# A stick-breaking branch moved ahead of the first gate, with paced weight sums, in a hybrid decoder layer

## The chip, the cores and the metric

The kernel runs on one core of a Trainium2 chip. The metric is device time in microseconds of one execution; the median of several runs is compared. TensorE (PE) multiplies matrices, VectorE (DVE) and ScalarE (ACT) do elementwise work, GpSimd (POOL) and SyncE (SP) mostly start DMAs here.

## The reference

One layer for 512 tokens of width 1024 in float32. A combined projection of `x` feeds three causal token mixers and three gates; the gated sum goes through an output projection and a LayerNorm, and an MLP with a gated extra embedding and a second LayerNorm follows:

```python
o_da = diff_attention(...)            # 4 heads, two softmax maps each
o_sb = stick_breaking_attention(...)  # 8 heads
o_dl = dilated_attention(...)         # 3 groups of 4 heads
g = jax.nn.sigmoid(gates).reshape(B, S, N_BRANCHES, D)
merged = (g[:, :, 0] * (o_da @ w_branch_da) + g[:, :, 1] * (o_sb @ w_branch_sb)
          + g[:, :, 2] * (o_dl @ w_branch_dil))
x = layer_norm(DEEPNORM_ALPHA * x + merged @ w_out, ln1_g, ln1_b)
c = jnp.square(jax.nn.relu(x @ w_up)) @ w_down
ple = jax.nn.sigmoid(x @ w_ple_gate) * (p @ w_ple)
x = layer_norm(DEEPNORM_ALPHA * x + c + ple, ln2_g, ln2_b)
```

The part of differential attention that the change touches, for every head and block of 128 queries:

```python
prob = jax.nn.softmax(logits, axis=-1)
w = prob[:, :, 0] - lam * prob[:, :, 1]
o = einsum(w, v)
o = o * lax.rsqrt(jnp.mean(jnp.square(o), axis=-1, keepdims=True) + RMS_EPS) * norm_g * (1 - lam_init)
```

## The kernel before, in words

**Products in three parts.** A float32 product is made of three matmuls of a faster type: every operand is split into a high part (a cast) and a low part (the rest), and high x high, high x low and low x high are summed in PSUM. Each 128x1024 chunk of weights is therefore loaded on SP's queue into `raw` (7 buffers), cast by ScalarE into `wh` (line 212) and subtracted by VectorE into `wl` (line 214); `wh` and `wl` have 6 buffers each. `pump` keeps these stages ahead of the matmuls that read them.

**Products with fewer multiplications.** The dilated values, the three gates, the gate of the extra embedding and most of the MLP use a two-by-two scheme of seven products in place of eight (Winograd's). It needs sums of blocks of weights and of activations. The sums of weights (`vsum`, `msum`, `gsum`, `usum`, `dsum`) are made in device memory by DMAs of 512 KB on POOL's queue, some of which add into their target: `sum_steps` yields 200 of them, eight for each group, up to four groups taking turns. The sums of activations are "forms": `value_forms` makes them for the dilated values from loads called `xr` (line 347), `mixer_forms` for the gates from loads also called `xr` (line 331); each makes eight such loads.

**Items.** TensorE's work is a list of items, each 12 to 24 matmuls with an evacuation `ev`. Items 0 to 64 are projections and values (`t_item`, `v_items`, `value_pair`); `last_plain` is 65. Then come the first gate (`gate_alone`, 14 items, line 575 ff.), the stick-breaking branch (`branch_items(1)`, 8 items, line 634 ff.), the second gate and the dilated branch, the third gate and the differential branch, the output projection, the extra embedding and the MLP, 298 items in all. The gate of a branch is a sigmoid (`gate_sig`, line 499), called one item ahead of the branch item (`pre`); the branch item's `ev` multiplies it by the branch product from PSUM (line 651). The first branch starts the sum `merged`, the others add to it.

**What runs between items.** The attention heads are generators. `step` advances those that are active, once per item and once more in the middle of projections and values; a head may start when the PSUM banks that the active ones declare leave room. All eight stick-breaking heads come first, then dilated and differential ones. Before the last item of the first gate the loop calls `step` until no head is left:

```python
if n == branch_at[1] - 1:
    while active or waiting:
        step()
```

`mixer_forms` is started at `last_plain - 5`. `split_oT(i)` splits a branch's attention outputs two items before the branch. The weight sums are issued by a credit: every item adds its size times a rate (2.6 up to `last_plain`, then 1.4, none around the output projection, later 0.42), and each whole unit issues one sum. An order derived from this program by a planner, which models times and hands out buffers, is what the engines run; each engine then works in that order. Most 128x512 tiles come from one pool of 46 buffers (`slot`), PSUM has 2 banks `mm` and 6 banks `at`.

**A block of differential attention** (`da_block`): logits of two maps, bias and maximum (line 1583), two exponentials with row sums (1589), reciprocals of the sums, one times lambda (1592, 1593), the second map scaled (1594), the first scaled and added (1595). Three steps later the result is transposed (1600) and copied, two steps later multiplied by the values (1614) and the squares summed (1618). After the last block of a head: `pow` on POOL (1624), scaling (1627), transposes (1633), `oT`.

Of the kernel before, what the change touches and what calls it, by code (L numbers as in the profile page):

```python
# [55 lines left out]
def trunk(tc, a, out):  # L56
    nc = tc.nc
    es = ExitStack()
    with es:
# [335 lines left out]
        def value_pair(nv):  # L395
# [6 lines left out]
            for p in (2, 1, 7, 6, 4, 5, 3):  # L402
                for r in range(2):
# [20 lines left out]
                    def ev(ps, p=p, r=r):  # L424
# [14 lines left out]
                        else:  # L439
                            o = V["dl_v", 2, r + 2 * (p == 5)] = slot("dl_v") if p == 4 else s[7, r]  # L440
                            nc.vector.scalar_tensor_tensor(o, s[7, r], -1.0, ps, op0=OP.mult, op1=OP.subtract)
                    item(cs[p] if r else [], mm, ev, need=cs[p], bank=bank, size=0.5)

        def v_items(nv, name, g):
            cs = [chunk(a["wv"][nv, c].rearrange("p k n -> p (k n)"), 1024) for c in range(4)]
            for tt in range(4):
# [11 lines left out]
                def ev(ps, tt=tt):  # L458
# [8 lines left out]
                    else:  # L467
                        t = slot(name)
                        cp(t, ps)
                        V[name, g, tt] = t  # L470
                item(cs if tt == 3 else [], mm, ev, need=cs)

        nt, nv = 2, 0
# [63 lines left out]
        def seven(forms, operand, bank_of, done):  # L537

            cs = {}
            for p in (2, 1, 7, 6, 4, 5, 3):  # L540
                for r in range(2):
# [19 lines left out]
                    if p == 5:  # L561
                        bank_of.get("sums", set()).add(len(items))
                    item(cs[p] if r else [], mm, ev, need=cs[p], bank=bank, size=0.5)

        msum = [[[dram.tile([P, 1024], F32, name=f"msum{n}_{m}_{i}") for i in range(4)] for m in range(2)]
# [68 lines left out]
        def branch_items(i, behind=()):  # L634
            behind = list(behind)
            for half in range(2):
                cs = [chunk(a["wb"][i, half, c].rearrange("p k n -> p (k n)"), 1024) for c in range(2)]
                for tt in range(4):
                    def mm(ps, tt=tt, cs=cs):
                        q = slice(tt * P, tt * P + P)  # L640
                        for k in range(4):
                            c = cs[k // 2]
                            n = slice(k % 2 * 512, k % 2 * 512 + 512)
                            h, lo = oTs[4 * i + k]
                            nc.tensor.matmul(ps, h[:, q], c["h"][:, n], start=k == 0, stop=False)  # L645
                            nc.tensor.matmul(ps, h[:, q], c["l"][:, n], start=False, stop=False)  # L646
                            nc.tensor.matmul(ps, lo[:, q], c["h"][:, n], start=False, stop=k == 3)  # L647

                    def ev(ps, tt=tt, half=half):
                        g = sg.pop((i, tt, half))  # L650
                        nc.vector.tensor_mul(g, g, ps)
                        if i == 1:
                            merged[tt, half] = g
                        else:
                            nc.vector.tensor_add(merged[tt, half], merged[tt, half], g)

                    def pre(tt=tt, half=half):
                        sg[i, tt, half] = gate_sig(i, tt, half)
                    item(cs if tt == 3 else [], mm, ev, need=cs, bank=at_bank, size=0.5)
                    items[-1]["pre"] = pre  # L660
                    if half and behind:
                        behind.pop(0)()
# [15 lines left out]
        last_plain = len(items)  # L678
        gate_alone(0, 1)
        branch_at = {1: len(items)}  # L680
        branch_items(1)
        for n, i in ((1, 2), (2, 0)):
            gate_chain(n, i)
            branch_at[i] = len(items)
            branch_items(i, () if i else [lambda k=k: turn_item(k) for k in range(4)])
# [255 lines left out]
        def sum_steps():  # L941
# [36 lines left out]
            todo.extend(up_steps(gsum[m], a["wg"][m]) for m in range(2))  # L978
            for m in range(ND):
                todo.append(up_steps(usum[m], a["wu"][m]))  # L980
                if m < ND - 1:
                    todo.append(down_steps(m))
            run = []
            while todo or run:
                while todo and len(run) < 4:
                    run.append(todo.popleft())
# [581 lines left out]
        da_po = {}  # L1568
        da_ss = {}
        da_left = {}  # L1570

        def da_block(hd, qb):
# [15 lines left out]
            for m in range(2):  # L1588
                e = nc.scalar.activation(lg[m], lg[m], AF.Exp, bias=mx[:, m:m + 1], accum_out=ssum[:, m:m + 1])
                last_exp[0] = getattr(e, "ins", e)  # L1590
            r = small("rr", 2)
            nc.vector.reciprocal(r, ssum)
            nc.vector.tensor_mul(r[:, 1:2], r[:, 1:2], lam)
            nc.vector.tensor_scalar(lg[1], lg[1], r[:, 1:2], None, op0=OP.mult)
            nc.vector.scalar_tensor_tensor(lg[0], lg[0], r[:, 0:1], lg[1], op0=OP.mult, op1=OP.add)
            for _ in range(3):
# [20 lines left out]
            ss = da_ss[hd]  # L1617
            nc.scalar.activation(scr, po[:, qs], AF.Square, accum_out=ss[:, qb:qb + 1])
            da_left[hd] -= 1
            if da_left[hd] == 0:  # L1620
                yield

                nc.vector.tensor_scalar(ss, ss, 1.0 / P, EPS, op0=OP.mult, op1=OP.add)
                nc.gpsimd.tensor_tensor(ss, ss, mhalf.to_broadcast([P, 4]), OP.pow)
                yield
                on = slot("on")
# [188 lines left out]
        sum_steps_ = sum_steps()  # L1815
        RATES = 2.6, 1.4
        credit = 0.0
        plain_left[0] = last_plain
        forms_at = last_plain - 5
        freed = 8  # L1820
        prev = None
        for n, it in enumerate(items):
            if n == v_from[0]:
                pending.append(value_forms())
            if n == forms_at:
                pending.append(mixer_forms())
            if n == branch_at[1] - 1:
                while active or waiting:
                    step()
# [28 lines left out]

            if 12 <= n < wout_at - 6:
                credit += it["size"] * (RATES[0] if n < last_plain else RATES[1])  # L1860
            elif n > ple_at + 14:
                credit += 0.42
            while credit >= 1:
# [141 lines left out]
```

## Time and profile before

| | |
|---|---|
| median of 3 runs | 1070.77 us (1067.01 to 1071.44) |
| profiled execution | 1073.48 us, span 1071.8 us |
| TensorE busy | 1046.1 us, 98% |
| VectorE busy | 764.1 us, 71% |
| ScalarE busy | 576.8 us, 54% |
| POOL busy | 179.5 us, 17% |
| read from and written to device memory | 251.21 MB, 106.98 MB |

The span runs from the first to the last instruction of the profiled execution. A row of waits names the instruction that waited, what released it, and the time in total. In a timeline a row is start, duration, engine, line, operation and operands, and in brackets the idle time before it with its releaser. Matmuls overlap, so the distance between starts is their pace, not the duration. Source lines are those of the kernel before.

### The profile page before, as it was taken

What the parts mean: (1) busy time and instruction counts of PE and PEld (TensorE: products, weight loads), DVE (VectorE), ACT (ScalarE), POOL (GpSimd) and SP (SyncE); (2) the same over time, 40 slices, a digit from 0 to 9 for tenths busy, and PEclk for the clock granted to TensorE, in tenths of its full rate; (3) what the DMA queues carried; (4) which work ended last, traced back from release to release, by engine and by line L of the source; (5) the groups of instructions that cost most, each with busy time, mean ns of one, the idle gap of its engine ahead of it and who ended that gap; (6) DMA issues with size and microseconds to landing.
All of it is one profiled execution on the core that took longest, in us unless ns stands there. A gap on an engine that the chain in (4) does not pass through costs nothing.

```text
span 1071.8 us, 15018 instructions
## 1 busy us (share of the span) xinstructions
PE 1046.1 (98%) x5474; PEld 889.5 (83%) x5474; DVE 764.1 (71%) x1352; ACT 576.8 (54%) x982; POOL 179.5 (17%) x271
## 2 busy tenths in 40 slices
PE   9999999999999999898999999999999999999997
PEld 6887788878888788786888888888999989989885
DVE  6887667639864656985466664789677867877976
ACT  6675445426434544665362633585656565566741
POOL 0002322332322433021121130000111010100000
PEclk9999999998999999898999999999999999999999
DMA  8348987998999999387599993248999879857612
GB/s 312 112 168 252 230 266 204 289 311 241 362 270 256 321 267 321 115 252 266 153 289 302 320 348 101 79 125 299 262 313 285 288 220 288 270 182 240 195 41 79
DMA packets 72761, 254.32 MB, mean 237 GB/s; under 512 B 8968, under 2 KB 9880, under 8 KB 72688
## 3 DMA queue, kind: packets, MB, share of 16 engines
q0 software_dynamic: 32464, 116.21, 41.1%
q1 hardware_dynamic: 39648, 136.24, 36.4%
q8 instruction: 43, 0.70, 0.2%
q10 hardware_dynamic: 576, 0.92, 0.2%
q14 instruction: 30, 0.25, 0.1%
HBM read 251.21 MB, written 106.98 MB: 334 GB/s over the span
## 4 chain that ended last, share of the span: by engine, by line
PE 82%; DMA 10%; DVE 5%; issue 1%; ACT 1%; POOL 0%; DVEq 0%; SPq 0%; POOLq 0%; ACTq 0%
PE mm L87 8%; PE mm L89 8%; PE mm L88 8%; PE at L1131 4%; PE at L1132 4%; PE at L1133 4%; DMA msum<-in_wgm_dram 4%; PE at L552 3%; PE at L553 3%; PE at L554 3%; PE at L645 2%; PE at L646 2%; PE at L647 2%; DMA msum<-msum 2%; PE mm L452 2%; PE mm L454 2%
## 5 line engine op out<-in xcount | busy, mean ns | idle before, releaser
L214 DVE TENSOR_TENSOR wl<-raw,wh 128x1024 fp32r<-128x1024 f32 x251 | 305.5, 1223 | 135.8 <-ACT wh L212 133.6
L212 ACT CAST wh<-raw 128x1024 fp32r<-128x1024 f32 x251 | 263.3, 1051 | 253.9 <-PE mm L88 123.5
L87 PE MATMUL mm<-xhT,wh 128*128 128x512 f32 x304 | 121.1, 398 | 1.0 <-DVE da_qb L101 1.0
L89 PE MATMUL mm<-xhT,wl 128*128 128x512 f32 x304 | 119.2, 392 | 0.1
L88 PE MATMUL mm<-xlT,wh 128*128 128x512 f32 x304 | 118.9, 391 | 0.0
L1131 PE MATMUL at<-wh,hh 128*128 128x512 f32 x188 | 73.7, 392 | 0.0
L1132 PE MATMUL at<-wl,hh 128*128 128x512 f32 x188 | 73.7, 392 | 0.0
L87 PE MATMUL mm<-x1hT,wh 128*128 128x256 f32 x256 | 73.6, 288 | 0.0
L1133 PE MATMUL at<-wh,hl 128*128 128x512 f32 x188 | 73.1, 389 | 0.0
L88 PE MATMUL mm<-x1lT,wh 128*128 128x256 f32 x256 | 72.3, 283 | 0.0
L89 PE MATMUL mm<-x1hT,wl 128*128 128x256 f32 x256 | 71.8, 283 | 0.0
L87 PEld LDWEIGHTS mm<-xhT,wh 128*128 128x128 f32 x304 | 57.2, 188 | 12.7 <-PE at L1600 1.2
L89 PEld LDWEIGHTS mm<-xhT,wl 128*128 128x128 f32 x304 | 57.1, 188 | 12.6 <-DVE wl L214 0.5
L88 PEld LDWEIGHTS mm<-xlT,wh 128*128 128x128 f32 x304 | 57.1, 188 | 10.4
L87 PEld LDWEIGHTS mm<-x1hT,wh 128*128 128x128 f32 x256 | 48.8, 191 | 4.7 <-ACT up L1065 3.0
L88 PEld LDWEIGHTS mm<-x1lT,wh 128*128 128x128 f32 x256 | 48.8, 191 | 1.5
L968 POOL DMA_DIRECT2D usum<-in_wu_dram x32 | 27.8, 868 | 127.4 <-DVE wl L214 102.2
L89 PEld LDWEIGHTS mm<-x1hT,wl 128*128 128x128 f32 x256 | 48.6, 191 | 0.0
L1133 PEld LDWEIGHTS at<-wh,hl 128*128 128x128 f32 x188 | 35.3, 188 | 7.7
L1131 PEld LDWEIGHTS at<-wh,hh 128*128 128x128 f32 x188 | 35.5, 189 | 6.0
L1132 PEld LDWEIGHTS at<-wl,hh 128*128 128x128 f32 x188 | 35.5, 189 | 5.5
L968 POOL DMA_DIRECT2D dsum<-in_wd_dram x28 | 24.8, 886 | 86.4 <-DVE wl L214 72.0
(554 smaller groups left out, 2679.5 us busy)
## 6 DMA issues: line engine op xcount, KB each, us to landing
usum<-in_wu_dram POOLq DMA_DIRECT2D x48, 512.0 KB, 9.6
dsum<-in_wd_dram POOLq DMA_DIRECT2D x42, 512.0 KB, 10.6
raw<-in_wt_dram SPq DMA_DIRECT2D x38, 512.0 KB, 7.8
msum<-in_wgm_dram POOLq DMA_DIRECT2D x36, 512.0 KB, 14.2
raw<-usum SPq DMA_DIRECT2D x32, 512.0 KB, 5.3
raw<-dsum SPq DMA_DIRECT2D x28, 512.0 KB, 5.2
raw<-in_wd_dram SPq DMA_DIRECT2D x25, 512.0 KB, 4.5
raw<-msum SPq DMA_DIRECT2D x24, 512.0 KB, 7.7
```

The lines of the kernel that those rows point to most:

```text
L87: nc.tensor.matmul(ps, wh, xh, start=start, stop=False, skip_group_check=True)
L88: nc.tensor.matmul(ps, wh, xl, start=False, stop=False, skip_group_check=True)
L89: nc.tensor.matmul(ps, wl, xh, start=False, stop=stop, skip_group_check=True)
L212: i = nc.scalar.copy(h, raw)
L214: i = nc.vector.tensor_sub(lo, raw, h.bitcast(F32))
L552: nc.tensor.matmul(ps, h[:, q], c["h"][:, n], start=go, stop=False, skip_group_check=True)
L553: nc.tensor.matmul(ps, h[:, q], c["l"][:, n], start=False, stop=False, skip_group_check=True)
L554: nc.tensor.matmul(ps, lo[:, q], c["h"][:, n], start=False, stop=end, skip_group_check=True)
L968: i = nc.gpsimd.dma_start(o, i, accum_op=OP.add, max_dma_last_dim=4096)
L1131: nc.tensor.matmul(ps, h[:, q], c["h"][:, s], start=go, stop=False, skip_group_check=True)
L1132: nc.tensor.matmul(ps, h[:, q], c["l"][:, s], start=False, stop=False, skip_group_check=True)
L1133: nc.tensor.matmul(ps, lo[:, q], c["h"][:, s], start=False, stop=end, skip_group_check=True)
```

## The change

- The stick-breaking branch's eight items stand ahead of the first gate. Their product is copied from PSUM by ScalarE into `b1` tiles, with the `mm` banks in place of `at` banks; the gate's sigmoid and the multiplication (`first_gate`) come later, one each in the third to tenth items of the second gate. The drain of the attention heads moves with the end of the first gate, `mixer_forms` starts at `last_plain - 1`, `split_oT` of the stick-breaking heads two items before item 65.
- Every item carries its own rate of weight sums: 2.5 for projections, 1.4 for values, 0.5 for the paired dilated values, 1.2 for gates, 1.5 for branches, 1.0 elsewhere, up to 12 items into the output projection; from 7 items into the extra embedding on 0.56 per item. The groups of the MLP's sums come in another order, and at most two take turns once nine or fewer groups are waiting.
- The two maps are combined without normalising the first: the second is scaled by lambda times the ratio of the row sums and added in one operation. The reciprocal of the first row sum enters as the scale of the squares and as a factor of the output rows.

```diff
@@ value_pair / v_items / seven / branch_items: rates
+                    items[-1]["rate"] = 0.5
...
+                items[-1]["rate"] = 1.4
...
+                    items[-1]["rate"] = 1.2
...
@@ branch_items
                     def ev(ps, tt=tt, half=half):
+                        if i == 1:
+                            t = slot("b1")
+                            nc.scalar.copy(t, ps)
+                            merged[tt, half] = t
+                            return
                         g = sg.pop((i, tt, half))
                         nc.vector.tensor_mul(g, g, ps)
-                        if i == 1:
-                            merged[tt, half] = g
-                        else:
-                            nc.vector.tensor_add(merged[tt, half], merged[tt, half], g)
+                        nc.vector.tensor_add(merged[tt, half], merged[tt, half], g)
...
-                    item(cs if tt == 3 else [], mm, ev, need=cs, bank=at_bank, size=0.5)
-                    items[-1]["pre"] = pre
+                    item(cs if tt == 3 else [], mm, ev, need=cs, bank=None if i == 1 else at_bank, size=0.5)
+                    items[-1]["rate"] = 1.5
+                    if i != 1:
+                        items[-1]["pre"] = pre
...
         last_plain = len(items)
-        gate_alone(0, 1)
+        for it in items:
+            it.setdefault("rate", 2.5)
+        def first_gate(tt, half):
+            g = gate_sig(1, tt, half)
+            nc.vector.tensor_mul(merged[tt, half], merged[tt, half], g)
+
         branch_at = {1: len(items)}
         branch_items(1)
+        gate_alone(0, 1)
+        gated_at = len(items)
         for n, i in ((1, 2), (2, 0)):
             gate_chain(n, i)
+            if n == 1:
+                for j, th in enumerate([(tt, half) for half in range(2) for tt in range(4)]):
+                    items[gated_at + 2 + j]["pre"] = lambda th=th: first_gate(*th)
...
@@ sum_steps
-            for m in range(ND):
-                todo.append(up_steps(usum[m], a["wu"][m]))
-                if m < ND - 1:
-                    todo.append(down_steps(m))
+            for kind, m in ("u0", "u1", "d0", "u2", "u3", "d1", "d2", "u4", "u5", "d3", "d4", "u6", "u7", "d5", "d6"):
+                m = int(m)
+                todo.append(up_steps(usum[m], a["wu"][m]) if kind == "u" else down_steps(m))
             run = []
             while todo or run:
-                while todo and len(run) < 4:
+                while todo and len(run) < (4 if len(todo) > 9 else 2):
...
@@ da_block
-            r = small("rr", 2)
-            nc.vector.reciprocal(r, ssum)
-            nc.vector.tensor_mul(r[:, 1:2], r[:, 1:2], lam)
-            nc.vector.tensor_scalar(lg[1], lg[1], r[:, 1:2], None, op0=OP.mult)
-            nc.vector.scalar_tensor_tensor(lg[0], lg[0], r[:, 0:1], lg[1], op0=OP.mult, op1=OP.add)
+            if hd not in da_rr:
+                da_rr[hd] = small("rr", 4)
+            r = da_rr[hd][:, qb:qb + 1]
+            r1 = small("r1", 1)
+            nc.vector.reciprocal(r1, ssum[:, 1:2])
+            nc.vector.reciprocal(r, ssum[:, 0:1])
+            nc.vector.scalar_tensor_tensor(r1, r1, lam, ssum[:, 0:1], op0=OP.mult, op1=OP.mult)
+            nc.vector.scalar_tensor_tensor(lg[0], lg[1], r1, lg[0], op0=OP.mult, op1=OP.add)
...
-            nc.scalar.activation(scr, po[:, qs], AF.Square, accum_out=ss[:, qb:qb + 1])
+            nc.scalar.activation(scr, po[:, qs], AF.Square, scale=r, accum_out=ss[:, qb:qb + 1])
...
                 nc.gpsimd.tensor_tensor(ss, ss, mhalf.to_broadcast([P, 4]), OP.pow)
+                nc.vector.tensor_mul(ss, ss, da_rr[hd])
...
@@ main loop
-        RATES = 2.6, 1.4
-        forms_at = last_plain - 5
+        forms_at = last_plain - 1
...
-            if n == branch_at[1] - 1:
+            if n == gated_at - 1:
                 while active or waiting:
                     step()
...
-            if 12 <= n < wout_at - 6:
-                credit += it["size"] * (RATES[0] if n < last_plain else RATES[1])
-            elif n > ple_at + 14:
-                credit += 0.42
+            if 12 <= n < wout_at + 12:
+                credit += it["size"] * it.get("rate", 1.0)
+            elif n > ple_at + 6:
+                credit += 0.56
```

More of the change, by code (lines that the diff above doesn't have):

```diff
@@ L1569, in trunk @@
         da_ss = {}
+        da_rr = {}
         da_left = {}
```

## The prediction

> **What bounds the kernel now.** I read the page first, then TensorE's own waits, then its instructions in time around each wait.
>
> ```profile
> span 1071.8 us, 15018 instructions
> ## 1 busy us (share of the span) xinstructions
> PE 1046.1 (98%) x5474; PEld 889.5 (83%) x5474; DVE 764.1 (71%) x1352; ACT 576.8 (54%) x982; POOL 179.5 (17%) x271
> ```
>
> TensorE is busy for 98% of the span and the change takes no matmul away. So only what it loses can be won: the time that it waits, and the time that it then runs slowly. TensorE's waits, in total, times and longest:
>
> ```profile
> PE mm L420 <- ACT dl_q L285: 4.3, 1, 4.3
> PE at L1600 <- DVE lg L1595: 3.4, 2, 2.9
> PE at L1633 <- DVE on L1627: 2.7, 1, 2.7
> PE at L1614 <- DVE wT L98: 2.1, 1, 2.1
> PE at L1740 <- DVE L L1721: 1.6, 1, 1.6
> ```
>
> The timeline of TensorE (start, duration, in brackets the idle time before) shows what follows such a wait.
>
> ```profile
> 243.69 0.82 PE L420 MATMUL mm<-wh,xhT 128*128 128x512 f32 x1 [4.29 <-ACT dl_q L285]
> ...
> 248.53 0.39 PE L422 MATMUL mm<-wh,xlT 128*128 128x512 f32 x1
> ...
> 450.55 1.11 PE L1600 MATMUL at<-ident,lg 128*128 128x128 f32 x4 [2.94 <-DVE lg L1595]
> ...
> 456.59 0.45 PE L552 MATMUL at<-wh,xhT 128*128 128x512 f32 x1
> ...
> 493.99 1.84 PE L1614 MATMUL at<-da_v,wT 128*128 128x128 f32 x8 [2.07 <-DVE wT L98]
> 498.48 1.09 PE L1633 MATMUL at<-ident,on 128*128 128x128 f32 x4 [2.66 <-DVE on L1627]
> ...
> 504.06 0.58 PE L647 MATMUL at<-wh,oTl 128*128 128x512 f32 x1
> 504.48 0.40 PE L645 MATMUL at<-wh,oTh 128*128 128x512 f32 x1
> 504.71 0.39 PE L646 MATMUL at<-wl,oTh 128*128 128x512 f32 x1
> ```
>
> Before 504.48 the matmuls start 0.42 us apart, after it 0.23 us: half speed after a wait, for some time. The first stretch (243.69 to 248.53) and the second (450.55 to 456.59) end in the same way. I price a slow stretch at half its length:
> - W1, value pair: 4.29 + 4.84/2 = 6.7 us.
> - W2, first dilated heads (L1740): 1.6 us, no slow stretch counted.
> - W3, first gate begins: 2.94 + 6.04/2 = 6.0 us.
> - W4, attention's end: 2.07 + 2.66 + (504.48 - 493.99 - 2.66)/2 = 8.6 us.
>
> Together 22.9 us, which is all that I let the change win.
>
> The Trainium skill ("TensorE: Matmul & The Clock Gate", Part 1) says that the clock falls to half after an idle window of about 3.4 us. By that rule W3 and W4 would cost their waits alone, and the sum would be 4.29 + 2.4 + 1.6 + 2.94 + 4.73 = 16.0 us. The rows do not agree with it: half speed stands behind waits of 2.07 and 2.94 us.
>
> **The change, part by part.** Items are the planned pieces of TensorE work; I number them from 0. Projections are 0 to 64, and every item lets the attention generators make a step (projections and values two).
>
> *Branch ahead of the gate (W4).* A block of the differential attention takes 3 steps from its logits to its transposes, 2 more to its product, and the last of a head 4 more to the final transposes. Counted along the loop, the last block (head 3, block 3) starts in item 75, which is the 11th of the gate's 14 items now. The last gate item then forces the eight steps that are missing, with nothing between them; that is where 493.99 and 498.48 stand. With the branch's 8 items in front, item 75 is the gate's 3rd item and the final transposes fall in its 12th, so no step is forced. Between two steps then lie 12 matmuls x 0.23 = 2.8 us, more than either wait of W4, and the final transposes come four steps behind the product. All of W4 goes: 8.6 us (ends: 0 if the planner, which sets each engine's order itself, bunches the tail again; 8.6).
>
> *Forms moved (W3).* The mixer's forms begin in item 64, not 60, with their 8 loads on POOL's queue, behind four items' more sums. Their distance to the gate that reads them stays (the first is read 6 items after it is made, 5 now), so the loads have the same time to land. What made W3:
>
> ```profile
> 433.00:451.00 18.00, 14.56 (x68) 11.63 (x68) 17.37 (x45) 14.19 (x31) 0.21 (x1) 0.97 0.29 99
> ```
>
> The columns are TensorE, its weight loads, VectorE, ScalarE, POOL, the clock, the DMA share. VectorE is full (17.37 of 18 us): forms, softmax blocks and the last projections' evacuations meet, and head 2's last block gets its combination late. In the new order the forms are eight steps later, among branch and first gate items, away from those evacuations. They meet blocks 2 and 3 of head 3 instead. Costs of a 128x512 pass, and what the new combination drops:
>
> ```profile
> L651 DVE TENSOR_TENSOR graw<-graw,at x24: 680/687/689, 504.7 to 645.8; 128x512 f32<-128x512 f32 x24
> L618 ACT COPY graw<-at x12: 574/584/590, 526.5 to 606.3; 128x512 f32<-128x512 f32 x12
> L1594 DVE TENSOR_SCALAR lg<-lg,rr x16: 280/415/491, 352.4 to 487.7; 128x128 f32<-128x128 f32 x4, 128x256 f32<-128x256 f32 x4, 128x384 f32<-128x384 f32 x4, 128x512 f32<-128x512 f32 x4
> ```
>
> The forms are 16 passes x 0.69 = 11 us on VectorE. Over the five items that issue them TensorE has some 5 x 2.8 + 3 (attention, estimated) = 17 us; weight splits, evacuations and the two blocks ask for about 12 more of VectorE. It falls up to 6 us behind, and block 3 has three items (8 us) from start to transposes. So W3 goes, and a smaller wait may come near the gate's 6th item: between 0 and 6 us with its slow stretch. I take 2, nearer the lower end since the evacuations are gone, and win 4.0 of 6.0.
>
> *Branch evacuation.* Eight ScalarE copies (0.58) replace eight VectorE products from PSUM (0.69); the products come back as SBUF passes of about the same 0.69 in items 89 to 96, with the eight sigmoids. VectorE thus gets 5.5 us back over eight items (27 us) of the second gate. The four splits of the stick-breaking output move from item 77 to 63: 4 x 0.69 = 2.8 us of VectorE, in front of two projections (14 us). In the branch two `mm` banks take turns, so a copy may be a whole item (2.8 us) late; behind it in ScalarE's queue are weight casts that are up to six chunks early. All this at nothing; bounds 0 to 8 x 0.6 = 5 us lost. The branch's outputs hold 8 more of 46 buffers; the allocations give a highest demand of about 49 in items 71 to 75, where before has 50 in item 65.
>
> *Combination in one operation.* It drops 16 x 0.415 = 6.6 us of VectorE and adds small operations, about half of that. It shortens the way to the transposes by 0.3 us per block, on the path only in W3 and W4, which are counted whole. The first normalisation on the output rows adds a 128x4 product per head, between `pow` and the output scaling; in W4 that stands among gate items: at nothing.
>
> *Paced sums (W1, W2).* A sum is a 512 KB DMA on POOL's queue. W1: VectorE's first `fr` waited for the `xr` loads behind the sums, and ScalarE's casts and `dl_q` behind it.
>
> ```profile
> 170.04 3.31 POOL L970 DMA_DIRECT2D msum<-in_wgm_dram  x4
> ...
> 216.09 0.52 POOL L970 DMA_DIRECT2D msum<-msum  x1 [3.20 <-DMA msum<-in_wgm_dram]
> ...
> 229.00 0.54 POOL L347 DMA_DIRECT2D xr<-in_xT_dram  x1 [3.33 <-PE at L1555]
> 230.26 0.54 POOL L347 DMA_DIRECT2D xr<-in_xT_dram  x1 [0.72 <-DMA msum<-msum]
> ...
> 230.26 7.93 DMA xr<-in_xT_dram
> DVE fr L370 <- DMA xr<-in_xT_dram: 10.5, 1, 10.5
> L87 PE MATMUL mm<-xhT,wh 128*128 128x512 f32 x80 | 31.4, 392 | 0.0
> ```
>
> From 170.04 to 216.09 POOL issues 20 sums, 2.3 us each. The last row (of 165.1 to 237.7) is ten projections, 7.3 us each; at 2.5 sums per item that is a sum per 2.9 us. By item 29, where the loads are planned, 7 x 2.5 + 4 x 1.4 + 7 x 2.5 = 40 sums are out, now 18 x 2.6 = 46. So the queue is shorter. But the load at 229.00 waits for a buffer that a stick-breaking head frees (PE at L1555), which does not move. The fifth load, which `fr` needs first, can go at 229.5 instead of 230.26. At worst it lands as slowly as now (7.93): 0.7 us won; at best W1 goes. I take half: 3.3 us.
>
> W2: VectorE waited for the differential tables.
>
> ```profile
> 290.38 15.07 DMA sh<-rv
> DMA to landing us min/median/max: 4.1/10.5/19.2
> ```
>
> Between items 33 and 46 the change issues 0.25 sums per item where 1.3 go now, so this load meets few of them; 15.07 need only fall by 1.6. W2 goes: 1.6 us (ends 0 and 1.6).
>
> The sums left out go later: by the loop's count 149 stand at the first MLP item, now 167, and the last comes at item 265, now 253.
>
> ```profile
> 700.00:950.00 250.00, 249.95 (x1587) 225.43 (x1585) 195.56 (x252) 157.86 (x249) 26.76 (x38) 1.00 0.84 261
> q0 software_dynamic: 32464, 116.21, 41.1%
> ```
>
> A sum costs 0.411 x 1071.8 / 116.21 x 0.524 MB = 2.0 us of all 16 engines. 18 more are 36 us. Over those 250 us the DMA share would go from 0.84 to 0.98 if all fell there. The shortest distance from a sum's issue to the load that reads it is 8 items (14 now), about 22 us, and loads run 13 chunks ahead of their use. At nothing.
>
> **Sum.** 8.6 + 4.0 + 3.3 + 1.6 = 17.5 us. The profiled execution took 1073.48 (span 1071.8), 2.7 above the median of 1070.77; 1073.5 - 17.5 = 1056.0 for such a run, and from the median 1070.8 - 17.5 = 1053.3.
>
> **The rivals.**
> - A: the waits only move. W3 returns whole at the first gate's forms and W1 stays. For it: VectorE's full stretch and the row at 229.00. Against: the evacuations are gone. 8.6 + 1.6 = 10.2 won: 1060.6.
> - B: everything goes, 22.9 won: 1047.9. Against: the buffer at 229.00.
> - C: the change does not do what it says. The planner bunches attention's tail again, W1 and W3 stay: only W2 goes, 1069.2. For it: 498.48 is followed at once by a branch matmul, although the last gate item is written between them, so the planner does move work. Against: it moves matmuls ahead of a late tail, which shortens the wait.
> - D, slower: the MLP's DMA. If demand over those 250 us exceeds what the queues give, a sum lands late and SP's loads, which stand in order, stop behind it. It decides once the lateness passes the 13 chunks' lead (about 36 us). At 0.98 x 250 = 245 us of work, a cost 30% above mine gives 319 - 250 - 36 = 33 us of waiting: 1053.3 + 33 = 1086. Against: TensorE kept 249.95 of 250 us at 0.84.
>
> **How the numbers follow.** My forecast 0.50, A 0.18, B 0.12, C 0.08, D or another loss 0.12. The likeliest time is 1053. The forecast and B and A lie from 1047.9 to 1060.6; with the bounds of the unknown costs (1 us below B, and up to 5 us lost in the branch's banks above A) the range is 1047 to 1066, which leaves out C and D. A measurement of this kernel can tell about 0.5% (5.4 us) from no change: below 1065.4 is faster. Forecast, A and B are faster (0.80), C is the same (0.08), D slower (0.12).
>
> **What would show it.** Right: no TensorE wait at L1633 or L1614 over 1 us, and final transposes with gate matmuls on both sides; W2's row gone; `fr` waiting less than 10.5 us; branch 1 matmuls ahead of the gate's. Wrong in a step: a wait at L1600 in the first gate over 3 us (A); a wait on `b1` copies in the branch; POOL's `xr` issues still ending after 235 us. My prediction fails as a whole if TensorE shows new waits after 700 us on `wh` chunks whose loads come from `usum` or `dsum` (D).

## The result, and the profile after

The changed kernel takes 1052.77 us (median; 1051.91 to 1053.95), the kernel before 1070.3 us in the same comparison. The ratio is 0.9842, with a 95% interval of 0.9818 to 0.9866: 17.5 us faster. The forecast was 1053.

The page of the changed kernel (its profiled execution took 1053.95 us, 1.2 above its median):

```profile
span 1052.0 us, 15035 instructions
...
PE 1037.5 (99%) x5474; PEld 883.7 (84%) x5474; DVE 763.5 (73%) x1356; ACT 582.9 (55%) x990; POOL 177.7 (17%) x271
```

With the same 5474 matmuls TensorE is busy for 1037.5 us where it was for 1046.1. I put these 8.6 us down to matmuls that no longer run at half clock (the granted clock, averaged over the span, went from 0.987 to 0.997). The rest of the span's 19.8 us is waiting that is gone. TensorE's longest waits after (total, times, longest), beside one of 1.3 us at the program's start that both kernels have:

```profile
PE mm L648 <- DVE da_klb L101: 1.1, 1, 1.1
PE at L1720 <- DVE r L1714: 1.0, 1, 1.0
PE at L131 <- ACT da_ka L122: 0.8, 2, 0.6
```

W2, W3 and W4 are not there. Of W1, 0.2 us are left at its place (L420), and two waits of 0.6 us stand shortly behind it (250.08 and 251.19). By stages (TensorE, weight loads, VectorE, ScalarE, POOL, the granted clock, DMA share, GB/s), first before, then after:

```profile
200.00:250.00 50.00, 45.71 (x209) 37.94 (x208) 28.15 (x45) 17.04 (x26) 13.92 (x22) 0.93 1.05 280
395.00:440.00 45.00, 44.88 (x241) 38.15 (x241) 29.09 (x93) 22.65 (x54) 12.98 (x17) 1.00 0.95 279
440.00:475.00 35.00, 31.56 (x150) 26.26 (x148) 31.53 (x73) 22.73 (x54) 4.68 (x7) 0.90 0.56 164
475.00:520.00 45.00, 40.27 (x176) 32.87 (x175) 26.04 (x42) 20.03 (x34) 6.20 (x10) 0.89 0.72 235
```

```profile
200.00:250.00 50.00, 49.38 (x233) 42.34 (x231) 32.28 (x65) 18.86 (x35) 11.81 (x17) 1.00 0.94 270
395.00:440.00 45.00, 41.88 (x220) 34.75 (x219) 32.49 (x107) 24.80 (x61) 13.75 (x20) 1.00 0.92 257
440.00:475.00 35.00, 35.00 (x182) 29.61 (x181) 27.04 (x68) 24.80 (x59) 2.69 (x4) 1.00 0.40 141
475.00:520.00 45.00, 45.00 (x208) 37.40 (x207) 34.84 (x44) 29.26 (x39) 8.38 (x11) 1.00 0.90 262
```

The value pair (200 to 250), the stretch around the first gate (440 to 475) and attention's end (475 to 520) were short of TensorE work and ran below full clock; after, all three are at 1.00. One stretch gives a little back: 395 to 440, where TensorE now stands for 45.00 - 41.88 = 3.1 us at full clock.

Attention's end, TensorE's timeline after:

```profile
494.95 0.39 PE L556 MATMUL mm<-wh,xlT 128*128 128x512 f32 x1
495.18 0.60 PE L1654 MATMUL at<-ident,on 128*128 128x128 f32 x4
495.54 0.48 PE L554 MATMUL mm<-wh,xhT 128*128 128x512 f32 x1
```

The last transposes (L1654, L1633 of the kernel before) stand between gate matmuls, with no idle time.

### The profile page after: what moved, and what is told of

Read it like the earlier page. It is cut to its first block, busy times and chain, and to the rows that moved or that the text cites. A ratio compares the mean times of both kernels' runs of the same rounds, so it can differ in the third digit from the quotient of the medians.

```text
span 1052.0 us, 15035 instructions
## 1 busy us (share of the span) xinstructions
PE 1037.5 (99%) x5474; PEld 883.7 (84%) x5474; DVE 763.5 (73%) x1356; ACT 582.9 (55%) x990; POOL 177.7 (17%) x271
## 4 chain that ended last, share of the span: by engine, by line
PE 84%; DMA 9%; DVE 3%; ACT 2%; issue 1%; POOL 0%; SPq 0%; DVEq 0%; POOLq 0%; ACTq 0%
PE mm L87 8%; PE mm L89 7%; PE mm L88 7%; PE at L1147 4%; PE at L1148 4%; PE at L1149 4%; DMA msum<-in_wgm_dram 4%; PE at L556 3%; PE at L555 3%; PE at L554 3%; PE mm L453 2%; PE mm L455 2%; PE mm L454 2%; DMA gsum<-gsum 2%; PE at L89 1%; PE at L88 1%
## 5 line engine op out<-in xcount | busy, mean ns | idle before, releaser
L87 PE MATMUL mm<-xhT,wh 128*128 128x512 f32 x304 | 121.1, 398 | 0.0
L87 PE MATMUL mm<-x1hT,wh 128*128 128x256 f32 x256 | 73.6, 288 | 0.0
L87 PEld LDWEIGHTS mm<-xhT,wh 128*128 128x128 f32 x304 | 57.2, 188 | 11.6 <-issue 0.4
L87 PEld LDWEIGHTS mm<-x1hT,wh 128*128 128x128 f32 x256 | 48.8, 191 | 4.7 <-ACT up L1081 2.8
```

The source lines that it names most:

```text
L87: nc.tensor.matmul(ps, wh, xh, start=start, stop=False, skip_group_check=True)
```

## The experiments

Medians in us; the kernel before took 1070.1 beside the first four, 1070.6 beside the next four and 1070.0 beside the last four.

### The change in three parts

**The sums alone** (`e1_rates_only`): the kernel before with the new rates and order of sums, nothing else.

```diff
+                    items[-1]["rate"] = 0.5
...
-            if 12 <= n < wout_at - 6:
-                credit += it["size"] * (RATES[0] if n < last_plain else RATES[1])
+            if 12 <= n < wout_at + 12:
+                credit += it["size"] * it.get("rate", 1.0)
...
```

> The kernel before with the paced sums alone (item rates, order of the MLP's groups, two groups at a time at the end); the branch stays behind the gate and the maps are normalised as before. Theory 'parts add up': the sums remove the waits in the value pair (6.7 us with the slow stretch, L420) and at the first dilated heads (1.6 us, L1740) and nothing else: 1070.3 - 8.3 = 1062.0 us; the waits at L1600, L1614 and L1633 stay. Rival 'the move gives room for all': the sums alone bring under 3 us, because a later load only shifts the wait.

1062.25 us, ratio 0.9927 (0.9907 to 0.9946), 7.9 us won. The waits that are left are those of the first gate and of attention's end, nearly unchanged:

```profile
PE at L1605 <- DVE lg L1600: 3.4, 2, 2.9
PE at L1638 <- DVE on L1632: 3.1, 1, 3.1
```

So the sums take away W1 and W2, and only those.

**The order alone** (`e2_move_only`): the changed kernel with the sums and the map combination of before; what remains is the branch ahead of the gate and the later forms.

```diff
...
-            if 12 <= n < wout_at + 12:
-                credit += it["size"] * it.get("rate", 1.0)
+            if 12 <= n < wout_at - 6:
+                credit += it["size"] * (RATES[0] if n < last_plain else RATES[1])
...
```

> The kernel after with the sums' rates and order of before and the maps of before: the branch ahead of the gate alone. Theory 'parts add up': the waits at L1614 and L1633 go whole (8.6 us) and the one at L1600 (6.0 us) for the most part: 1070.3 - 8.6 - 5 = 1056.7 us; the wait of L420 stays (4.3 us and half clock behind it). Rival: the tail of attention is bunched again by the planner, under 3 us won, a wait at L1633 or its successor over 2 us stays.

1059.84 us, ratio 0.9902 (0.9883 to 0.9922), 10.3 us won. W1 stays (4.5 us at L420), W3 and W4 are gone, and small waits of 0.3 to 0.8 us come at L131 and L648, as in the changed kernel:

```profile
PE mm L420 <- ACT dl_q L285: 4.5, 1, 4.5
...
PE mm L648 <- DVE da_klb L101: 0.8, 1, 0.8
```

**The map combination alone** (`e3_maps_only`): the kernel before with the new combination and the factor on the output rows.

```diff
...
-            nc.vector.tensor_scalar(lg[1], lg[1], r[:, 1:2], None, op0=OP.mult)
-            nc.vector.scalar_tensor_tensor(lg[0], lg[0], r[:, 0:1], lg[1], op0=OP.mult, op1=OP.add)
+            nc.vector.scalar_tensor_tensor(lg[0], lg[1], r1, lg[0], op0=OP.mult, op1=OP.add)
...
                 nc.gpsimd.tensor_tensor(ss, ss, mhalf.to_broadcast([P, 4]), OP.pow)
+                nc.vector.tensor_mul(ss, ss, da_rr[hd])
```

> The kernel before with the maps combined in one operation and the first normalisation on the output rows, nothing else. Theory 'parts add up': VectorE loses about 3 us of work, the waits at L1600 and L1614 become shorter by some tenths: 1070.3 - 0 to 1 us. Rival: the operation that falls away stood on the path of L1600's wait; if it brings that wait under 2 us, the half-speed stretch behind it goes too and 3 to 5 us are won.

1079.76 us, ratio 1.0086 (1.0065 to 1.0107): **9.6 us slower**, where the theory had 0 to 1 us won and the rival 3 to 5. There is one long new wait of TensorE, 8.8 us, and its cause can be followed back through two engines. TensorE, then VectorE, then POOL, in time:

```profile
419.13 0.61 PE L1702 MATMUL at<-r,fold 128*128 128x32 f32 x2 [8.78 <-DVE nm L1689]
```

```profile
404.52 0.16 DVE L1627 TENSOR_SCALAR ms<-ms 128x4 f32<-128x4 f32 x1
404.63 0.17 DVE L1668 TENSOR_SCALAR nm<-st 128x4 f32<-128x4 f32 x1
416.79 0.16 DVE L1629 TENSOR_TENSOR ms<-ms,rr 128x4 f32<-128x4 f32 x1 [11.98 <-POOL ms L1628]
416.87 0.28 DVE L1685 CUSTOM_DVE_ANT_0 L<-at,shf 128x128 f32<-128x128 f32 x1
...
418.91 0.17 DVE L1689 TENSOR_SCALAR nm<-st 128x4 f32<-128x4 f32 x1
425.93 0.69 DVE L1632 TENSOR_TENSOR on<-at,ms 128x512 f32<-128x512 f32 x1
```

```profile
...
411.39 0.71 POOL L331 DMA_DIRECT2D xr<-in_xT_dram  x1 [3.06 <-DMA dsum<-in_wd_dram]
...
415.14 0.55 POOL L970 DMA_DIRECT2D dsum<-dsum  x1
415.70 1.05 POOL L1628 TENSOR_TENSOR ms<-ms,mhalf 128x4 f32<-128x4 f32 x1
```

The new product, 0.16 us long, stands in VectorE's order directly behind the first half of a dilated head. It needs the power, the power's input is ready at 404.7, but POOL still has the rest of the mixer's loads and two sums to issue, most of them held until an earlier transfer ends, and reaches the power at 415.70. VectorE stands 11.98 us; the dilated head's second half (L1685) is behind it in the queue, and TensorE behind that. In the kernel before the power is as late and nobody minds:

```profile
415.08 1.72 POOL L1624 TENSOR_TENSOR ms<-ms,mhalf 128x4 f32<-128x4 f32 x1
...
417.34 0.69 DVE L1627 TENSOR_TENSOR on<-at,ms 128x512 f32<-128x512 f32 x1
```

There its first reader on VectorE is `on`, whose row has no idle time ahead of it: VectorE had done the dilated head (L1680 of the kernel before, at 408.79) in the meantime.

**What the combination costs in the new order** (`e10_after_oldmaps`): the changed kernel with the old combination, the e3 edit backwards.

```diff
...
-            nc.vector.scalar_tensor_tensor(lg[0], lg[1], r1, lg[0], op0=OP.mult, op1=OP.add)
+            nc.vector.tensor_scalar(lg[1], lg[1], r[:, 1:2], None, op0=OP.mult)
+            nc.vector.scalar_tensor_tensor(lg[0], lg[0], r[:, 0:1], lg[1], op0=OP.mult, op1=OP.add)
...
                 nc.gpsimd.tensor_tensor(ss, ss, mhalf.to_broadcast([P, 4]), OP.pow)
-                nc.vector.tensor_mul(ss, ss, da_rr[hd])
```

> The changed kernel with the maps combined and normalised as before: what the map combination is worth in the new order. By the forecast's own step (some 0.3 us less in each of 16 blocks, all of it beside TensorE, and in the new order no wait of TensorE for the product although VectorE stands 7.3 us at it in four): 1052.5 to 1053.5 us. Rival (it costs the 9 us here too that it cost alone): 1043.5 us, which could not be less than TensorE's own 1037.5 busy us. Second rival (it gains, as its parts removed from VectorE's full windows): 1055 us.

1052.99 us, ratio 0.9841 (0.9826 to 0.9857): the same as the changed kernel. The edit that costs 9.6 us alone costs nothing beside the others. So the parts are 7.9 and 10.3 us, together 18.2; with both, 1070.0 - 1053.0 = 17.0 were measured, and 17.5 with the combination.

### Why the combination is free in the new order

**Forms early** (`e4_forms_early`): the changed kernel with the mixer's forms, and with them their eight loads on POOL's queue, at their old place.

```diff
-        forms_at = last_plain - 1
+        forms_at = last_plain - 5
```

> The kernel after, but the gate's forms start at last_plain - 5 again, among the last projections. Theory 'VectorE was full there': the forms meet the last projections' evacuations again and a wait of 2 to 3 us at the transposes L1600's successor or nearby returns with a slow stretch: 1052.8 + 3 to 6 = 1056 to 1059 us. Rival 'the branch items give VectorE the room': the branch needs so little of VectorE that the forms' place is of no account: 1052 to 1054 us.

1063.53 us (1060.67 to 1066.63), ratio 0.9942 (0.9924 to 0.996): 10.8 us slower than the changed kernel, more than any theory had. But not at the first gate's transposes, where I looked for it (0.7 us there). The wait is that of e3, at the same instruction: TensorE, VectorE, POOL:

```profile
408.91 0.60 PE L1718 MATMUL at<-r,fold 128*128 128x32 f32 x2 [6.73 <-DVE nm L1705]
```

```profile
406.57 0.16 DVE L1645 TENSOR_TENSOR ms<-ms,rr 128x4 f32<-128x4 f32 x1 [9.82 <-POOL ms L1644]
```

```profile
393.16 4.58 POOL L331 DMA_DIRECT2D xr<-in_xT_dram  x6
399.39 0.72 POOL L331 DMA_DIRECT2D xr<-in_xT_dram  x1 [1.65 <-DMA gsum<-in_wg_dram]
403.29 0.71 POOL L331 DMA_DIRECT2D xr<-in_xT_dram  x1 [3.18 <-DMA usum<-in_wu_dram]
...
405.14 1.39 POOL L1644 TENSOR_TENSOR ms<-ms,mhalf 128x4 f32<-128x4 f32 x1
```

The eight loads are ahead of the power again. In the changed kernel none of them is in POOL's queue yet, and VectorE stands 3.95 us:

```profile
400.21 0.53 POOL L987 DMA_DIRECT2D gsum<-gsum  x1 [2.41 <-DMA gsum<-in_wg_dram]
400.76 1.05 POOL L1644 TENSOR_TENSOR ms<-ms,mhalf 128x4 f32<-128x4 f32 x1
```

A further 2.8 us in e4 are at its branch (L648): there a copy into `b1` comes late (L655, from 447.60), the wait that the prediction bounded at 0 to 5 us and that the changed kernel does not have.

**The product one step later** (`e9_maps_late` on e3, `e12_early_late` on e4, `e11_after_late` on the changed kernel): meant to take VectorE's stand away.

```diff
                 nc.gpsimd.tensor_tensor(ss, ss, mhalf.to_broadcast([P, 4]), OP.pow)
-                nc.vector.tensor_mul(ss, ss, da_rr[hd])
                 yield
+                nc.vector.tensor_mul(ss, ss, da_rr[hd])
                 on = slot("on")
```

> The kernel before with the map combination alone, as in the run that was slower at 1079.8 us, but with the 128x4 product of the two factors issued one step later, directly ahead of the 128x512 product that reads it. Theory (in that run VectorE stood 11.98 us at the product behind GpSimd's power, which lay in GpSimd's queue behind ten loads, and TensorE stood 8.8 us behind VectorE): one step later the power has been done, as it had in the kernel before, where the 128x512 product stood at 417.34 and the power ended at 416.80. The wait of 8.8 us goes, the others stay: 1079.8 - 8.8 less what the slow clock behind it cost (half of some 2 us) = 1069 to 1071 us. Rival (the combination itself costs, by its chain of reciprocals or by the normalisation on the rows): it stays at 1077 to 1081 us.

> The changed kernel with the mixer's weight forms queued four items earlier, as in the run at 1063.5 us, and the 128x4 product one step later. There TensorE stood 6.7 us at the fold, behind VectorE that stood 9.82 us at the product, behind GpSimd's power and nine loads; and 2.8 us at L648. Theory (the forms' place costs only through that product): 1063.5 - 6.7 - 1 = 1055 to 1057 us with the 2.8 us still there, 1053 without. Rival (the forms' earlier place costs by itself): 1061 to 1064 us.

> The changed kernel with the 128x4 product issued one step later, where VectorE no longer stands for GpSimd's power. VectorE stood 7.3 us in four there, of which 3.95 us at 401.85, shortly ahead of TensorE's waits of 1.0 at L1720 and 0.8 and 0.3 at L131. If those waits are late by that stand: 1050.5 to 1052 us. If they are not (the dilated head's own chain): 1052.8 us, no difference.

1078.6 us (ratio 1.0089, 1.0071 to 1.0106), 1064.35 us (0.9946, 0.9924 to 0.9967) and 1053.44 us (0.9847, 0.9833 to 0.9862): no difference in any of the three. By the numbers the rivals would have it, but the experiment did not do what it was for. VectorE in e9:

```profile
404.61 0.17 DVE L1668 TENSOR_SCALAR nm<-st 128x4 f32<-128x4 f32 x1
416.06 0.16 DVE L1630 TENSOR_TENSOR ms<-ms,rr 128x4 f32<-128x4 f32 x1 [11.28 <-POOL ms L1628]
...
425.19 0.69 DVE L1632 TENSOR_TENSOR on<-at,ms 128x512 f32<-128x512 f32 x1
```

The planner that sets each engine's order put the product where it had been, behind L1668 and nine microseconds ahead of `on`, though the two are now written one below the other. It places by its own model, not by the line, and so no run here has the product without the stand. That the stand causes the slowdown rests on the chain of rows in e3 and e4, on the kernel before (power as late, no product ahead of the dilated head, no wait) and on e10 against the changed kernel (loads elsewhere, product free); a run that removes it alone is missing. e11, where VectorE still stands 4.2 us, leaves open whether the 1 us waits at 395 to 440 hang on that stand. e10, which has no such product, narrows it: its profile has the waits at L131 (0.6 and 0.3 us) and at L648 (0.8 us), and none at L1720. So little more than the 1.0 us at L1720 can hang on it.

### What held the dilated values (W1) and the first heads (W2)

**POOL's order** (`e6_xr_on_sp`): the kernel before with the eight `xr` loads of the value forms on SP's queue, past POOL's sums.

```diff
-                i = nc.gpsimd.dma_start(t, xt[:, k, :])
+                i = nc.sync.dma_start(t, xt[:, k, :])
```

> The kernel before with the eight loads of the value forms on SP's queue in place of POOL's; the sums keep their rates. Theory 'POOL's order': the loads waited behind sums in POOL's queue; on SP they land some 5 to 10 us earlier and the wait at L420 goes (6.7 us): 1063.6 us. Rival 'buffers and bandwidth': buffers freed by the stick-breaking heads and full DMA engines set the landing; the wait stays within 1 us of 4.3: 1070 us. SP's own weight loads may be held behind these loads, which would show as waits of casts on raw.

1071.91 us, ratio 1.0012 (1.0001 to 1.0023); the wait at L420 is 6.4 us. The loads are issued at 214.71 to 222.5, where POOL issued them at 218.85 to 236.0, but they take 16.5 us to land (median, 21.6 at most; before 8.2 and 16.7), and the DMA share between 200 and 250 stays at 1.05 (the last column but one):

```profile
200.00:250.00 50.00, 43.59 (x194) 36.02 (x193) 26.10 (x42) 16.67 (x25) 8.58 (x13) 0.93 1.05 286
```

With the sums alone paced (e1) it is 0.90 and TensorE is busy for all 50 us. But the share is not what helped: from 205 to 235, where the loads are issued, it is the same, first in the kernel before, then in e1:

```profile
205.00:235.00 30.00, 30.00 (x142) 25.05 (x141) 13.24 (x20) 9.83 (x14) 5.91 (x11) 1.00 1.05 295
205.00:235.00 30.00, 30.00 (x142) 25.06 (x142) 16.39 (x25) 11.09 (x17) 8.71 (x13) 1.00 1.05 294
```

In e7, the next run, it is 1.03 over the whole 50 us, and W1 is gone. What differs is the work that stands ahead of the loads. In the kernel before and in e6 four steps that copy one sum into another (`msum<-msum`) are issued between 205 and 217 and take some 21 us each to land. In e1, e7 and the changed kernel no step of this kind is issued from 200 us to the last of the loads. Their loads take longer to land than before (13.3 to 14.4 us, median), but start at 214.0 to 214.4 in place of 218.85, and the second pass of `fr` (L363) begins at 237.1 to 239.3 in place of 244.19. In e6, with the four steps in flight beside the loads, it begins at 245.88. So passing the sums in the queue does not help while they are still in flight; having fewer of them issued ahead of the loads does. No run separates the number of the sums from the kind of their steps.

**The rates up to the pair** (`e7_rates_to_32`) and **in the pair** (`e8_pair_rate`): the kernel before with one or the other of the new rates. In e8 the sums left out are made up at a higher rate from the first gate on. In e7 six sums fewer stand ahead and are not made up, so some weights are read before their sums are complete; its time is that of a program without that dependency.

```diff
@@ e7
-                credit += it["size"] * (RATES[0] if n < last_plain else RATES[1])
+                credit += it["size"] * (1.4 if n in (19, 20, 21, 22) else 2.5 if n < 33 else RATES[0] if n < last_plain else RATES[1])
@@ e8
-                credit += it["size"] * (RATES[0] if n < last_plain else RATES[1])
+                credit += it["size"] * (0.5 if 33 <= n < 47 else RATES[0] if n < last_plain else 1.9)
```

> The kernel before with 2.5 sums per projection and 1.4 per value item up to item 32 alone, the old rates behind it. Theory: the shorter queue in front of the xr loads (about six sums fewer) removes the value pair's wait whole, as in the kernel after: 1070.3 - 6.7 = 1063.6 us, and the wait at L1740 stays at 1.6 us. Rival: only the sums that are left out during the value pair matter, since they compete for the DMA engines with the loads in flight: under 2 us won.

> The kernel before with 0.25 sums per item during the value pair (1.3 before), made up for after item 65 (1.9 for 1.4 at a time); the rates before the pair are the old ones. Theory: the xr loads are already queued when the pair begins, so the wait at L420 stays at 3 to 4.3 us, and the tables' wait at L1740 goes: 1070.3 - 1.6 = 1068.7 us. Rival: the wait at L420 goes too (1062 us), and then the pace during the pair was the cause of both.

e7: 1069.12 us (1066.37 to 1074.31), ratio 0.9985 (0.9967 to 1.0003). Its profiled execution took 1067.76 and shows no wait at L420: W1 is gone. Even so only 1.5 us are won, as the rival's number had it, and the interval includes none. W2 is 2.2 us with half clock behind it, and new waits of 1.0 and 0.8 us stand at 382.39 and 390.59 (L1600, L1614); why these came I have not followed. e8: 1077.47 us, ratio 1.0062 (1.0047 to 1.0077). The other way round: L420 stays (4.1 us), L1740 is gone. So by the waits, not by the times, W1 belongs to the rate before the pair and W2 to the rate in it; e1 has both. e8's loss is the mechanism of e3 once more, now with the old combination:

```profile
PE at L1633 <- DVE on L1627: 10.3, 2, 5.3
DVE on L1627 <- POOL ms L1624: 14.9, 2, 11.9
```

```profile
379.09 1.06 POOL L1624 TENSOR_TENSOR ms<-ms,mhalf 128x4 f32<-128x4 f32 x1
```

The power's input was there at 368.3; six sums stood between. The sums fell differently, and the power of a head ended up behind them.

### Attention's end (W4)

**No forced steps** (`e5_no_drain`): the kernel before without the loop that empties the attention ahead of the gate's last item; the branch stays behind the gate.

```diff
-            if n == branch_at[1] - 1:
-                while active or waiting:
-                    step()
```

> The kernel before without the forced steps at the end of the first gate: the last heads' remaining eight steps then run between the stick-breaking branch's items, one per item, and the branch stays behind the gate. Theory 'the forced steps made W4': the waits at L1614 and L1633 go with their slow stretch (8.6 us), the one at L1600 stays: 1070.3 - 8.6 = 1061.7 us. Rival 'the chain is too long whatever stands between': products, squares, pow and scaling still hold the final transposes, over 2 us of wait stays, under 4 us won.

1062.29 us, ratio 0.992 (0.9905 to 0.9935): 8.3 us won, and no wait at L1633. The waits at L420 (5.8) and L1600 (3.4) stay. W4 was the forced steps. That the 8.3 come so near the price of 8.6 is in part chance, since the medians hold other differences too: in e5's profiled execution the wait at L420 is 1.6 us longer, and no half clock follows the wait at L1600:

```profile
451.17 0.66 PE L1600 MATMUL at<-ident,lg 128*128 128x128 f32 x4 [2.93 <-DVE lg L1595]
```

```profile
451.17:461.17 10.00, 10.00 (x59) 8.82 (x60) 10.00 (x18) 4.36 (x11) 1.89 (x3) 1.00 0.57 185
```

The place of the same instructions in the two profiled executions gives W4 by itself. At the last block's transposes (L1600, 490.14 before, 487.93 in e5) e5 is 2.2 us ahead, at the first matmul of L1131 (776.5 and 765.5) 11.0 us. So 8.8 us were won in between, and the price stands. Leaving the forced steps out gives this part without moving the branch.

## Why the prediction was right, point by point

- **The bound, right.** Only waits and the half clock behind them could be won. The profiled spans differ by 19.8 us: the 22.9 us counted, less the 3.1 us of standing at 395 to 440. The rest cancels: 1.3 us of small waits remain at the value pair, and 1.5 us of other small ones are gone (0.96 at L87, 0.50 at L1600).
- **W4, 8.6 won: right**, in size (8.8 between the same instructions of e5) and in mechanism (the last transposes between gate matmuls).
- **W3, 4.0 of 6.0 won: too little, and its reason wrong.** No wait is left at the transposes of the first gate; the 2 us that I kept for one near its sixth item did not come there. And it is not the later forms that take W3 away: with the forms early (e4) those transposes wait for 0.7 us. It goes with the branch's items in front. Its price holds for one execution only: 3.0 of the 6.0 us are half clock, which did not follow the same wait in e5 and e7. What the later forms do is something that the prediction did not have: they keep eight loads out of POOL's queue ahead of a power that VectorE now waits for.
- **W1, 3.3 of 6.7 won: half its size.** The step that failed is the buffer: the load at 229.00 waited for a buffer of a stick-breaking head, and I took that buffer for a bound on the load behind it, which `fr` needs. After, one load still waits that way at 229, but it is the eighth, not the fourth:

```profile
214.26 1.67 POOL L347 DMA_DIRECT2D xr<-in_xT_dram  x3 [5.12 <-DVE wl L214]
216.18 0.54 POOL L347 DMA_DIRECT2D xr<-in_xT_dram  x1 [0.26 <-issue]
219.23 0.54 POOL L347 DMA_DIRECT2D xr<-in_xT_dram  x1 [2.51 <-DMA msum<-in_wgm_dram]
...
229.11 0.54 POOL L347 DMA_DIRECT2D xr<-in_xT_dram  x1 [3.07 <-PE at L1571]
```

The fifth goes at 219.23, 11.0 us earlier than before. The buffers come free at the same times (222.49 and 229.00 before, 222.80 and 229.11 after), but now the sixth and the eighth load wait for them, where the second and the fourth did; why, I have not followed. The prediction's bound at the bad end was wrong as well: the loads land more slowly than before (14.4 us in place of 8.2, median), and W1 goes since they start earlier.
- **W2, 1.6 won: right.** The tables' loads land after 5.2 to 8.6 us, where the slowest took 19.2, and e8 against e7 puts it on the rate in the pair:

```profile
DMA to landing us min/median/max: 5.2/6.7/8.6
```

- **Branch evacuation at nothing (0 to 5 lost): 1.1 us**, the branch's first item at L648, behind VectorE's evacuation of the last projections, not behind a `b1` copy. The other small new waits at 395 to 440 (L1720, L131) bring it to some 3; the prediction named none of them. The `b1` copies were no idle fear: with the forms early (e4) TensorE waited 2.8 us for one.
- **The combination at nothing: right for this kernel (e10), and wrong as it was argued.** I looked for the new product only in W4, "among gate items". There it costs nothing. I did not ask of heads 0 to 2 what stands behind it in VectorE's queue and ahead of the power in POOL's; alone the same edit costs 9.6 us (e3). Both queues had to be checked, and only the later forms made the answer come out right. VectorE's total fell by 1.8 us (763.5 against 765.3 in e10), not by some 3.3 (half of 6.6) as taken.
- **The MLP's sums at nothing: right.** The DMA share over the MLP went to 0.95, estimated 0.98, and TensorE keeps 249.95 of 250 us:

```profile
700.00:950.00 250.00, 249.95 (x1620) 227.19 (x1619) 194.00 (x248) 152.53 (x234) 38.08 (x56) 1.00 0.95 304
```

Rival D falls with this row, A with W1, C with the transposes at 495.18; B, everything goes, had the waits right and left out the 3.1 us.

The total came out 0.5 us from the 1053.3 worked out from the median, since errors met. What was won was taken too small by 5.4 us (W1 by 3.4, W3 by 2.0). Against that stand the 3.1 us of new waits, and some 2 us by which the profiled execution that the terms were read from lay further above its median (1073.48 to 1070.3) than the one after (1053.95 to 1052.77). The clock goes with this: the profiled execution before had a mean granted clock of 0.987, while most runs of the same kernel beside the experiments had 0.990 to 0.993. So the slow stretches were priced from an execution that had more of them than most.

## What to carry to other kernels

A small operation that reads another engine's result costs what stands ahead of that result in the other engine's queue, if something urgent is behind the reader: 0.16 us of product became 9.6 us, since POOL's queue held DMA issues that waited for transfers. Look at both queues for every instance of it, not for the last one only. Price an edit in the order that it will run in: the same one cost 9.6 us alone and nothing with the others, so tests of the parts one at a time would have thrown it out. And where a load lands late among background transfers, count those issued ahead of it and still in flight before changing the queue; the busy share of the DMA engines alone did not tell the good order from the bad.

## What the runs showed of the hardware

A wait of TensorE of about 2 us can halve its clock, but need not. In e7 it waited 2.19 us at L1740, and the granted clock (the last column but two) behind it was 0.50; the kernel before waited 1.61 us at the same place and its stretch 280 to 320 stayed at 1.00.

```profile
303.03 1.39 PE L1740 MATMUL at<-ident,L 128*128 128x128 f32 x7 [2.19 <-DVE L L1721]
```

```profile
303.00:305.00 2.00, 1.97 (x11) 1.72 (x12) 2.00 (x8) 1.58 (x7) 1.34 (x2) 0.74 1.02 322
305.00:307.00 2.00, 2.00 (x12) 2.00 (x11) 1.13 (x7) 0.00 (x0) 0.28 (x1) 0.50 1.03 328
```

The rule of the Trainium skill ("TensorE: Matmul & The Clock Gate", Part 1) that the prediction weighed, an idle window of about 3.4 us, does not agree with this row either. On the other side, 2.93 us at L1600 in e5 (shown there) left the clock at 1.00 for the next 10 us, and so did 2.94 us at the same transposes in e7 (448.45); in the kernel before, the clock behind that wait of 2.94 us was 0.50 from 450.55 to 456.55. The wait of 2.8 us at L648 in e4 cost no clock either. Every wait above 4 us in these runs (4.1 to 8.8) had half clock behind it. So between 2 and 3 us the length of a wait alone does not say whether half clock follows, and the price of a slow stretch read from one execution is not a fixed cost of its wait. The changed kernel's new waits, 1.1 us at most, cost no clock: 1.00 from 395 to 440.
